# One load instead of three ahead of the opening barrier, in a streaming row-mean on Trainium2

## Chip, cores, metric

The kernel runs on one core of a Trainium2 chip. The metric is device time in microseconds (us). Every run used below was in the fast state, at a granted clock of 1.0. The threshold is 2%.

## The reference

The input is 32 x 512 rows of 1024 floats, 67.11 MB. The output is one float per row.

```python
def reference(x, divisor):          # x: (32, 512, 1024) f32, divisor = 1024.0
    return (np.sum(x, axis=-1) / divisor).astype(np.float32)
```

## The kernel before

The 16384 rows are spread over 128 partitions. Nine tiles of up to 14 rows per partition (128x14x1024 floats, 7168 KB) go through three buffers. All loads are issued from the sync queue. The vector engine (DVE) sums each tile; the activation engine (ACT) takes some rows of the last ones. A tapering tail of small loads keeps the work after the last byte short.

```python
    main = [(14, 0)] * 6 + [(14, 4), (14, 6), (8, 4)]      # (rows, rows summed by ACT)
    bulk = ctx.enter_context(tc.tile_pool(name="bulk", bufs=3))
    # ...
    nc.gpsimd.memset(r, 0.0)
    # ...
    j = 0
    for rows, on_act in main:
        t = bulk.tile([P, 14, D], F32, name="t")
        load(t[:, :rows, :], x_main[:, j : j + rows, :])     # sync queue
        sums(res[:, j : j + rows], t, rows, on_act)
        j += rows
    # ... the tapering tail, scaling, two stores
```

A program has a first block, which ends with a barrier of all engines, and a body. A load in the body is issued after that barrier. The first three loads wait for nothing, since all three buffers are free, so a helper moves them from the body to the place in the first block just before the sync engine's drain:

```python
def start_loads_at_once(nc):
    first, body = nc.main_func.blocks[0], nc.main_func.blocks[1]
    loads = []
    for i in body.instructions:
        if i.engine == SP:
            if type(i).__name__ != "InstDMACopy" or (i.sync_info and i.sync_info.on_wait):
                break
            loads.append(i)
    # ... take them out of the body, then put them ahead of SP's drain:
    first.instructions = first.instructions[:at] + loads + first.instructions[at:]
```

Of the kernel before, what the change touches and what calls it, by code (L numbers as in the profile page):

```python
# [14 lines left out]
SP = mybir.EngineType.SP  # L15


def start_loads_at_once(nc):



    first, body = nc.main_func.blocks[0], nc.main_func.blocks[1]
    loads = []
    for i in body.instructions:
        if i.engine == SP:
            if type(i).__name__ != "InstDMACopy" or (i.sync_info and i.sync_info.on_wait):
                break
            loads.append(i)
    names = {i.name for i in loads}
    assert names  # L30
    body.instructions = [i for i in body.instructions if i.name not in names]
    at = next(
        k for k, i in enumerate(first.instructions) if i.engine == SP and type(i).__name__ == "InstDrain"
    )
    first.instructions = first.instructions[:at] + loads + first.instructions[at:]


def with_sync(i, on_wait=None, on_update=None):
# [29 lines left out]
def close_while_storing(nc, landed):  # L68


    body, end = nc.main_func.blocks[1], nc.main_func.blocks[-1]
    store = [i for i in body.instructions if i.engine == SP and type(i).__name__ == "InstDMACopy"][-1]
    (lane,) = store.sync_info.on_update
    drain = end.instructions[0]
    assert drain.engine == SP and type(drain).__name__ == "InstDrain"
    needs = {w.id: w for w in drain.sync_info.on_wait}
    assert needs[lane.id].wait_value > lane.update_value
    needs[lane.id] = dataclasses.replace(
        needs[lane.id], wait_value=needs[lane.id].wait_value - lane.update_value
    )  # L80

    (done,) = [w for w in store.sync_info.on_wait if w.ant_name.startswith("DVE_")]
    assert needs[done.id].wait_value == done.wait_value
    del needs[done.id]
    own = dict(sync_type="semaphore", id=landed.num, ant_name=landed.name)
    add = mybir.SyncUpdate(update_mode="sem-add-imm", update_value=16, **own)
    sub = mybir.SyncUpdate(update_mode="sem-sub-imm", update_value=16, **own)
    last = nc.sync.wait_ge(landed, 16).ins
    assert nc.main_func.blocks[-1].instructions[-1].name == last.name
    body.instructions = [i for i in body.instructions if i.name != store.name]  # L90
    end.instructions = [
        with_sync(drain, on_wait=tuple(needs.values())),
        with_sync(store, on_wait=(done,), on_update=(add,)),
        *end.instructions[1:-1],
        with_sync(last, on_update=(sub,)),
    ]


@with_exitstack
def kernel(  # L100
    ctx: ExitStack,
    tc: tile.TileContext,
    x: bass.AP,
    divisor: float,
    out: bass.AP,
):
    nc = tc.nc
    landed = nc.alloc_semaphore("landed")
    nc.at_finalize(start_loads_at_once)
    nc.at_finalize(latest_wait_first)  # L110
    nc.at_finalize(lambda nc: close_while_storing(nc, landed))
    xf = x.flatten_outer_dims()
    N, D = xf.shape
    P = nc.NUM_PARTITIONS
    scale = 1.0 / float(divisor)
    J = N // P
    assert J * P == N


    L = 8  # L120
    M = J - L
    x_main = bass.AP(tensor=x.tensor, offset=0, ap=[[M * D, P], [D, M], [1, D]])
    x_last = bass.AP(tensor=x.tensor, offset=P * M * D, ap=[[L * D, P], [D, L], [1, D]])
    o_main = bass.AP(tensor=out.tensor, offset=0, ap=[[M, P], [1, M]])
    o_last = bass.AP(tensor=out.tensor, offset=P * M, ap=[[L, P], [1, L]])


    main = [(14, 0)] * 6 + [(14, 4), (14, 6), (8, 4)]
    last = [(4, 2), (2, 1)]
    assert sum(n for n, _ in main) == M and sum(n for n, _ in last) == L - 2  # L130
    bulk = ctx.enter_context(tc.tile_pool(name="bulk", bufs=3))
    one = ctx.enter_context(tc.tile_pool(name="one", bufs=1))
    psum = ctx.enter_context(tc.tile_pool(name="junk", bufs=4, space=bass.MemoryType.PSUM))

    res = one.tile([P, M], F32, name="res")
    fin = one.tile([P, L], F32, name="fin")
    q = one.tile([P, L], F32, name="q")
    r = one.tile([P, L], F32, name="r")
    nc.gpsimd.memset(r, 0.0)  # L139

    def load(dst, src):
        tc.keep_in_program_order(nc.sync.dma_start(out=dst, in_=src))  # L142

    def act_sum(dst, src, by=1.0):
        n = src.shape[-1]
        junk = psum.tile([P, D], F32, name="junk")
        nc.scalar.activation(junk[:, :n], src, COPY, scale=by, accum_out=dst)  # L147

    def sums(dst, t, rows, on_act):
        d = rows - on_act  # L150
        for i in range(d, rows):
            act_sum(dst[:, i : i + 1], t[:, i, :])
        nc.vector.reduce_sum(out=dst[:, :d], in_=t[:, :d, :], axis=AX)  # L153
# [4 lines that stand above are left out]
        load(t[:, :rows, :], x_main[:, j : j + rows, :])  # L158
# [3 lines that stand above are left out]
    for rows, on_act in last:  # L162
        t = one.tile([P, rows, D], F32, name=f"t{rows}")
        load(t, x_last[:, j : j + rows, :])
        sums(q[:, j : j + rows], t, rows, on_act)
        j += rows


    c = 768
    row = one.tile([P, D], F32, name="row")  # L170
    load(row, x_last[:, j, :])
    act_sum(r[:, j : j + 1], row[:, c:], by=scale)
    nc.vector.reduce_sum(out=q[:, j : j + 1], in_=row[:, :c], axis=AX)  # L173



    a, b = 448, 704
    pa = one.tile([P, a], F32, name="pa")
    pb = one.tile([P, b - a], F32, name="pb")
    pc = one.tile([P, D - b + 2], F32, name="pc")  # L180
    load(pa, x_last[:, L - 1, :a])
    load(pb, x_last[:, L - 1, a:b])
    load(pc[:, : D - b], x_last[:, L - 1, b:])


    nc.gpsimd.tensor_scalar_mul(out=res, in0=res, scalar1=scale)  # L186
    tc.keep_in_program_order(nc.sync.dma_start(out=o_main, in_=res))

    act_sum(pc[:, D - b : D - b + 1], pa)
    nc.vector.reduce_sum(out=pc[:, D - b + 1 :], in_=pb, axis=AX)  # L190
    nc.vector.scalar_tensor_tensor(  # L191
        out=fin[:, : L - 1], in0=q[:, : L - 1], scalar=scale, in1=r[:, : L - 1], op0=MULT, op1=ADD
    )
    scaled = one.tile([P, D - b + 2], F32, name="scaled")
    nc.vector.tensor_scalar(  # L195
        out=scaled, in0=pc, scalar1=scale, scalar2=0.0, op0=MULT, op1=ADD, accum_out=fin[:, L - 1 :]
    )
    tc.keep_in_program_order(nc.sync.dma_start(out=o_last, in_=fin))
# [35 lines left out]
```

## Time and profile before

| | before |
|---|---|
| time, median of the first 3 runs | 161.70 us (161.69 to 161.78) |
| span in the profile | 160.1 us |
| DMA queue busy | 97.8% of 16 engines' span |
| vector engine busy | 75% |
| first reduction starts | 19.58 us |
| reductions of full tiles apart | 16.94 us, of which 15.09 busy |

The lines behind this table are in the prediction. In the view in order of time, a line gives start, duration, engine, source line, operation, output and input; the bracket at its end gives the idle time of the engine just before it and what ended that. Neighbouring lines of one kind are merged: "1.34 ... x3" are three issues, 1.34 us from the start of the first to the end of the last.

Some terms. An issue is the instruction with which the sync queue hands a load to the 16 DMA engines; what it hands over are descriptors. A packet is one record of data moved in the trace (57344 bytes in the full tiles). A completion packet is a record of 4 bytes; each load has 16 of them, taken here to be one per engine. A load has landed when the instruction that waits for it can start, so a landing is dated here by the start of the reduction. The drain (DRAIN) is the sync queue's last instruction before it waits at the barrier. The span runs from the first instruction in the profile to the end of the last.

### The profile page before, as it was taken

The page shows a single profiled execution, that of the slowest core. Times are in us where ns is not written, and L with a number is a line of the kernel's source. Part 1 is how long each engine was busy: PE and PEld are TensorE (multiplying, and loading weights), DVE is VectorE, ACT ScalarE, POOL GpSimd, SP SyncE. Part 2 cuts the span into 40 slices and gives each one's busy share as a digit, 9 for nine tenths or more (in the row PEclk, how much of TensorE's full clock was granted, in tenths as well). Part 3 has the DMA queues.
Part 4 walks back from the last instruction along what each step waited for, and adds up shares of the span by engine and source line. Part 5 has one row for each costly group of instructions (what it writes and reads, how often), then busy time and mean ns, then how long its engine had stood idle before and what let it go on. Part 6 is the DMA issues. An engine that isn't in the chain of part 4 may idle for free.

```text
span 160.1 us, 138 instructions
## 1 busy us (share of the span) xinstructions
DVE 119.9 (75%) x16; ACT 20.7 (13%) x39; POOL 0.8 (1%) x6
## 2 busy tenths in 40 slices
DVE  0000199968998699959995999599987990497985
ACT  3000000000000000000000000000007300491973
POOL 0000000000000000000000000000000000000010
DMA  8899999998899999998899999999799999999993
GB/s 301 387 458 458 458 458 458 458 430 358 358 458 458 458 458 458 458 458 387 358 401 458 458 458 458 458 458 430 315 401 458 458 458 458 393 393 405 415 402 104
DMA packets 2448, 67.18 MB, mean 419 GB/s; under 512 B 528, under 2 KB 912, under 8 KB 1040
## 3 DMA queue, kind: packets, MB, share of 16 engines
q1 hardware_dynamic: 2448, 67.18, 97.8%
HBM read 67.11 MB, written 0.07 MB: 419 GB/s over the span
## 4 chain that ended last, share of the span: by engine, by line
DMA 67%; DVE 29%; another core or an unknown queue 1%; SPq 1%; issue 0%; DVEq 0%
DMA t<-in_x_dram 45%; DVE res L153 28%; DMA row<-in_x_dram 22%; SPq L142 1%; DVE q L173 1%; DVE scaled L195 0%; DVE pc L190 0%; DVE fin L191 0%; DVEq L195 0%; DVEq L229 0%
## 5 line engine op out<-in xcount | busy, mean ns | idle before, releaser
L153 DVE TENSOR_REDUCE res<-t 128x14 f32<-128x14336 f32 (+3 forms) x9 | 114.4, 12716 | 37.9 <-DMA t<-in_x_dram 37.9
L147 ACT ACTIVATE junk<-t 128x1024 f32<-128x1024 f32 x17 | 17.2, 1011 | 135.2 <-DMA t<-in_x_dram 135.2
L153 DVE TENSOR_REDUCE q<-t 128x2 f32<-128x2048 f32 (+1 forms) x2 | 3.5, 1752 | 0.7 <-DMA t<-in_x_dram 0.7
L147 ACT ACTIVATION_READ_ACCUMULATOR junk<-t 128x1 f32 x17 | 3.2, 186 | 0.0
L147 ACT ACT_TABLE_LOAD x1 | 1.3, 1283 | 1.7 <-PEq L215 1.7
L186 POOL TENSOR_SCALAR res<-res 128x120 f32<-128x120 f32 x1 | 0.5, 512 | 150.5 <-DVE res L153 150.5
L173 DVE TENSOR_REDUCE q<-row 128x1 f32<-128x768 f32 x1 | 1.0, 953 | 0.1
L195 DVE TENSOR_SCALAR_CACHE_REDUCE scaled<-pc 128x322 f32<-128x322 f32 x1 | 0.5, 490 | 0.1
L147 ACT ACTIVATE junk<-pa 128x448 f32<-128x448 f32 x1 | 0.5, 547 | 0.1
L190 DVE TENSOR_REDUCE pc<-pb 128x1 f32<-128x256 f32 x1 | 0.4, 412 | 0.0
L147 ACT ACTIVATE junk<-row 128x256 f32<-128x256 f32 x1 | 0.4, 387 | 0.1
L191 DVE SCALAR_TENSOR_TENSOR fin<-q,r 128x7 f32<-128x7 f32 x1 | 0.2, 167 | 0.0
L147 ACT ACTIVATION_READ_ACCUMULATOR junk<-row 128x1 f32 x1 | 0.2, 187 | 0.0
L147 ACT ACTIVATION_READ_ACCUMULATOR junk<-pa 128x1 f32 x1 | 0.2, 186 | 0.0
L139 POOL MEMSET r<- 128x8 f32 x1 | 0.1, 104 | 1.3 <-POOLq L215 1.3
L215 POOL MEMSET const-bfloat16-1.0<- 128x1 bf16 x1 | 0.1, 101 | 0.0
L215 POOL MEMSET const-uint8-127<- 128x1 uint8 x1 | 0.1, 101 | 0.0
L215 POOL MEMSET const-float32-0.0<- 128x1 f32 x1 | 0.1, 99 | 0.2 <-issue 0.2
L215 POOL MEMSET const-float32-1.0<- 128x1 f32 x1 | 0.1, 98 | 0.0
L195 DVE DVE_READ_ACCUMULATOR scaled<-pc 128x1 f32 x1 | 0.1, 82 | 0.0
## 6 DMA issues: line engine op xcount, KB each, us to landing
t<-in_x_dram SPq DMA_DIRECT2D x8, 7168.0 KB, 35.7
t<-in_x_dram SPq DMA_DIRECT2D x1, 4096.0 KB, 28.5
t<-in_x_dram SPq DMA_DIRECT2D x1, 2048.0 KB, 33.0
t<-in_x_dram SPq DMA_DIRECT2D x1, 1024.0 KB, 35.0
row<-in_x_dram SPq DMA_DIRECT2D x1, 512.0 KB, 35.8
pa<-in_x_dram SPq DMA_DIRECT2D x1, 224.0 KB, 36.0
pc<-in_x_dram SPq DMA_DIRECT2D x1, 160.0 KB, 35.7
pb<-in_x_dram SPq DMA_DIRECT2D x1, 128.0 KB, 35.9
```

The source lines that it names most:

```text
L139: nc.gpsimd.memset(r, 0.0)
L142: tc.keep_in_program_order(nc.sync.dma_start(out=dst, in_=src))
L147: nc.scalar.activation(junk[:, :n], src, COPY, scale=by, accum_out=dst)
L153: nc.vector.reduce_sum(out=dst[:, :d], in_=t[:, :d, :], axis=AX)
L173: nc.vector.reduce_sum(out=q[:, j : j + 1], in_=row[:, :c], axis=AX)
L186: nc.gpsimd.tensor_scalar_mul(out=res, in0=res, scalar1=scale)
L190: nc.vector.reduce_sum(out=pc[:, D - b + 1 :], in_=pb, axis=AX)
L191: nc.vector.scalar_tensor_tensor(out=fin[:, : L - 1], in0=q[:, : L - 1], scalar=scale, in1=r[:, : L - 1], op0=MULT, op1=ADD)
L195: nc.vector.tensor_scalar(out=scaled, in0=pc, scalar1=scale, scalar2=0.0, op0=MULT, op1=ADD, accum_out=fin[:, L - 1 :])
L215: nc = _bacc.Bacc("TRN2", target_bir_lowering=False, num_devices=1)
```

## The change

The intent: let only load 1 stand ahead of the barrier. Loads 2 and 3 go back to the head of the body, so the sync engine reaches the barrier earlier and the other engines start earlier. The intent counts on load 2's data not moving anyway while load 1's keeps the DMA engines busy.

```diff
-def start_loads_at_once(nc):
+def start_first_load_at_once(nc):
     first, body = nc.main_func.blocks[0], nc.main_func.blocks[1]
-    loads = []
-    for i in body.instructions:
-        if i.engine == SP:
-            if type(i).__name__ != "InstDMACopy" or (i.sync_info and i.sync_info.on_wait):
-                break
-            loads.append(i)
-    names = {i.name for i in loads}
-    assert names
-    body.instructions = [i for i in body.instructions if i.name not in names]
+    load = next(i for i in body.instructions if i.engine == SP)
+    assert type(load).__name__ == "InstDMACopy" and not load.sync_info.on_wait
+    body.instructions = [i for i in body.instructions if i.name != load.name]
     # ...
-    first.instructions = first.instructions[:at] + loads + first.instructions[at:]
+    first.instructions = first.instructions[:at] + [load] + first.instructions[at:]
     # ... and the one call of the helper, by its new name
```

More of the change, by code (lines that the diff above doesn't have):

```diff
@@ L108 @@
     landed = nc.alloc_semaphore("landed")
-    nc.at_finalize(start_loads_at_once)
+    nc.at_finalize(start_first_load_at_once)
     nc.at_finalize(latest_wait_first)
```

## The prediction

> **What bounds the kernel now.** I read the page from the top: busy shares, the slices, the chain that ended last, and the groups; then the order of time on the vector engine, the stretches between landings, the waits of the queue that issues the loads, and at last the first microseconds, where the change sits.
>
> The busy shares and the chain first.
>
> ```profile
> span 160.1 us, 138 instructions
> DVE 119.9 (75%) x16; ACT 20.7 (13%) x39; POOL 0.8 (1%) x6
> q1 hardware_dynamic: 2448, 67.18, 97.8%
> DMA 67%; DVE 29%; another core or an unknown queue 1%; SPq 1%; issue 0%; DVEq 0%
> ```
>
> The reader is to see that the one DMA queue, q1, has its 16 engines busy 97.8% of the span while the busiest compute engine has 75%. The chain puts 29% on DVE, but that is a way in which it can be followed back, not a limit: it goes through a reduction that freed a buffer, and the buffer was free long before its new data was due. The next two views show this. First the reductions in order of time:
>
> ```profile
> 19.58 15.09 DVE L153 TENSOR_REDUCE res<-t 128x14 f32<-128x14336 f32 x1 [19.58 <-DMA t<-in_x_dram]
> 36.52 15.09 DVE L153 TENSOR_REDUCE res<-t 128x14 f32<-128x14336 f32 x1 [1.86 <-DMA t<-in_x_dram]
> ```
>
> A full tile takes 15.09 us to reduce and the next reduction starts 16.94 us after the one before (36.52 - 19.58). The 1.86 us between are a wait for the load. The stretches between landings say what the load does in that time:
>
> ```profile
> 0.00:4.00 4.00, 0.00 (x0) 1.28 (x1) 0.29 (x5) 1.00 0.89 301
> 4.00:19.58 15.58, 0.00 (x0) 0.00 (x0) 0.00 (x0) 1.00 1.04 453
> 19.58:36.52 16.94, 15.09 (x1) 0.00 (x0) 0.00 (x0) 1.00 1.00 433
> 36.52:53.46 16.94, 15.09 (x1) 0.00 (x0) 0.00 (x0) 1.00 1.00 433
> ```
>
> The last two columns are DMA share and GB/s. Between the first and second landing, and between the second and third, the DMA share is 1.00 at 433 GB/s: no hole. (The 1.04 before is an effect of counting a packet where it starts.) A tile of 7168 KB at 433 GB/s is 16.95 us, the cadence just seen. So from about 4 us on the kernel is a stream of data at a fixed rate. Only three things can set its time: when the stream starts, whether it ever runs dry, and the short tail after the last byte. A change to the opening can touch only the first two.
>
> Now the opening, in order of time:
>
> ```profile
> 0.00 1.34 SPq L142 DMA_DIRECT2D t<-in_x_dram  x3
> 0.32 0.10 POOL L215 MEMSET const-uint8-127<- 128x1 uint8 x1
> 1.74 1.28 ACT L147 ACT_TABLE_LOAD   x1 [1.74 <-PEq L215]
> 1.74 0.10 POOL L139 MEMSET r<- 128x8 f32 x1 [1.32 <-POOLq L215]
> ```
>
> Three issues stand back to back on the sync queue from 0.00 to 1.34 us. The other engines are done with their opening by 0.42 us and then wait at the barrier until 1.74. Last, what belongs to the barrier on the sync queue, from the view of its line:
>
> ```profile
> L215 SPq DRAIN  x1: 125/125/125, 1.4 to 1.4; - x1
> L215 SPq EVENT_SEMAPHORE  x1: 17/17/17, 1.7 to 1.7; - x1
> ```
>
> The sync engine is thus the last to arrive: its drain starts at 1.40 us, right after the third issue, and the barrier opens some 0.15 us after that drain has ended.
>
> **What the Trainium skill says.** The page "DMA: Bandwidth & Descriptors", section "Specifications", gives a fabric ceiling of 435 GB/s for the 16 engines; the trace agrees, with 433 GB/s between landings. The stream has no rate left to gain. The same page, section "Queues, rings and completion order", says that on each DMA engine the descriptors of a row are consumed in ring order. The trace agrees: the three loads, though issued within 1.34 us, are reduced from 19.58, 36.52 and 53.47 us on, one tile of data apart. The second load therefore moves no byte while the first is moving. The same page, section "Latency and other measured facts", gives about 600 ns to the first byte for a load issued from the sync queue. In the trace's records of single packets the first packet of the first load starts at 1.02 us, which is 0.64 us after its issue ended at 0.38.
>
> **The change part by part.** It computes nothing new and removes nothing. In the order of the sync queue it goes from "load 1, load 2, load 3, drain, barrier" to "load 1, drain, barrier, load 2, load 3". Four parts, with single durations from the trace's records.
>
> 1. Load 1. It stays the first instruction of the sync queue, from 0.00 to 0.38 us. Its first packet should start near 1.02 us as before: change 0.
>
> 2. The barrier. Two issues leave its front: load 2 from 0.43 to 0.87 and load 3 from 0.91 to 1.34 us. With the gaps that is 1.34 - 0.38 = 0.96 us. The drain should start at 0.44 instead of 1.40 us, end at 0.56, and the barrier let the engines go at about 0.78 instead of 1.74 us (1.74 - 0.96). The others arrive by 0.42 to 0.49 us (the pool engine's drain took 169 ns from 0.30), so the sync engine stays last, barely. What gains 0.96 us by this: the activation table load, 1.28 us, which would run from 0.78 to 2.06 instead of 1.74 to 3.02, and the memset of r, which is read at 157.6 us. The first activation runs at 121.2 us. DVE has nothing to do before the landing at 19.58. On the path that sets the end: 0.
>
> 3. Loads 2 and 3. Load 2 should be issued at about 0.78 us instead of 0.43: 0.35 us later. Load 3 follows 0.48 us after it, at about 1.26 instead of 0.91. Load 2's data is first wanted when the fastest DMA engine has done its share of load 1. The completion packets of load 1 in the records stand from 18.65 to 19.17 us, so load 2 must be in the ring by 18.65. With 0.64 us from end of issue to first packet it is there by 0.78 + 0.43 + 0.64 = 1.85 us: a margin of some 16.8 us, of which the change spends 0.35. For load 3 the margin is one tile more. On the path: 0.
>
> 4. All later loads wait for a reduction and a buffer, and those follow from the landings, which do not move: 0. The sum is 0.00 us on the path, against a shift of about 0.96 us for things that nobody waits for.
>
> **The rivals.**
>
> A. The first packets get faster. The 16 first packets (one on each DMA engine) start between 1.02 and 1.83 us and take 2.2 to 3.3 us, mean 2.89, where all later ones of 57344 bytes take 2.12. The last engine to get to its second packet does so at 4.38 us, the first at 3.85, and this spread of 0.53 us is still there in the completion packets at 18.65 to 19.17 us, and again one tile later. If writing the descriptors of loads 2 and 3, which falls into the same time, is what slows or staggers the first packets, moving them 0.35 us later could give some of it back: at most the 0.77 us of the first packets' excess, to 160.9 us. Against it: issues of later loads also fall into running packets and hardly touch them. Around the issues at 34.7, 51.6 and 68.6 us the mean packet takes 2.12 us, longer by 0.01 us at most. And load 2 would in the new order still be issued before the first packet starts. That a stream which begins shows the latency of its first reads once is the plainer reading. I give this a gain of 0.1 to 0.4 us one chance in six.
>
> B. The moved loads get in the way. Their descriptors would now be written from about 1.4 to 2.4 us, wholly within the first packets instead of partly ahead of them. If that is what stretches packets, those of the engine that is last could end 0.1 to 0.3 us later, which shifts every landing: to 161.9 or 162.0. The same small effect around later issues speaks against it; some 0.02 us for two issues is what it would support. One chance in eight.
>
> C. The barrier takes the place of the issues and holds load 2 up for long: a late arrival of another engine, or a stall on the way into the main body. It would have to last over 16 us to be seen, and the other engines are at the barrier within half a microsecond. This would make nothing of the time: 161.7.
>
> D. The start of the span shifts, as what is counted first changes. The span begins with the issue of load 1 in the kernel before, and load 1 is in the same place after. The measured 161.7 us is 1.6 us above the span of 160.1, an offset outside it that I take to stay. No change.
>
> **Range and chances.** The central reckoning is 161.7 + 0.00 us. Rival A weighs slightly more than B: 0.17 x (-0.25) + 0.12 x 0.2 is -0.02 us, so 161.7 stays. The three runs before span 0.09 us; another chip or another hour may add two or three tenths. The range 161.2 to 162.1 holds A's and B's usual sizes and that scatter. Two per cent are 3.2 us, four times all that A could return even in full, and no rival reaches that on the slow side. I keep one per cent for faster and two for slower, the latter for some disturbance at start that I do not see.
>
> **What would show it right or wrong.** Right: the first reduction starts at 19.58 us within 0.1, the next ones 16.94 us apart with waits of 1.86; the table load starts near 0.78 us; the sync queue's drain comes after one issue, near 0.44; the DMA share stays at 1.00 between landings. Rival A or B: the first reduction starts 0.1 us or more earlier or later and all later landings move by the same amount, at an unchanged cadence. Rival C: a share under 1.00 between the first and second landing. The prediction would be wrong if the cadence itself moved, for which I see no mechanism, or if the first packet of load 1 started at another time than 1.02 us.

## The result, and the profile after

| | before | after |
|---|---|---|
| median of 4 runs each | 161.69 us | 161.75 us |
| lowest to highest | 161.69 to 161.78 | 161.66 to 161.82 |
| ratio after / before | | 1.0002, 95% interval 0.9985 to 1.0019 |

A ratio here is the mean time of one kernel's fast runs over the mean of the other's fast runs of the same rounds, so it is not quite the ratio of the medians.

The span and the DMA queue of the changed kernel:

```profile
span 160.3 us, 138 instructions
q1 hardware_dynamic: 2448, 67.18, 97.7%
```

The opening of the changed kernel in order of time, with the first two reductions:

```profile
0.00 35.17 SPq L136 DMA_DIRECT2D t<-in_x_dram  x4
0.79 1.28 ACT L141 ACT_TABLE_LOAD   x1 [0.79 <-PEq L209]
0.80 0.10 POOL L133 MEMSET r<- 128x8 f32 x1 [0.38 <-POOLq L209]
19.73 15.09 DVE L147 TENSOR_REDUCE res<-t 128x14 f32<-128x14336 f32 x1 [19.73 <-DMA t<-in_x_dram]
36.65 15.09 DVE L147 TENSOR_REDUCE res<-t 128x14 f32<-128x14336 f32 x1 [1.83 <-DMA t<-in_x_dram]
```

The table load starts at 0.79 us where it stood at 1.74: the barrier opens 0.95 us earlier. Nothing comes of it. The first reduction starts at 19.73 us, which is 0.15 later than in the profile of before, and the second again waits for its load.

The stretches between landings, changed kernel (length, busy time of DVE, ACT and POOL, clock, DMA share, GB/s):

```profile
19.58:36.52 16.94, 15.09 (x1) 0.00 (x0) 0.00 (x0) 1.00 1.00 433
36.52:53.46 16.94, 15.09 (x1) 0.00 (x0) 0.00 (x0) 1.00 1.00 433
```

Rate and share are those of before: no hole was made. The barrier's part on the sync queue, from the view of its line:

```profile
L209 SPq DRAIN  x1: 140/140/140, 0.4 to 0.4; - x1
L209 SPq EVENT_SEMAPHORE  x1: 17/17/17, 0.7 to 0.7; - x1
```

The drain now follows the first issue, at 0.4 us instead of 1.4. By the trace's records of single instructions load 2 is issued at 0.80 us (0.43 before) and load 3 at 1.18 (0.91 before).

One thing in this pair does not fit "nothing moves": the 0.15 us of the first reduction. It runs through to the end (span 160.3 against 160.1). So there were two theories to test.

**Margin theory.** The place of loads 2 and 3 does not matter while they are issued before load 1 leaves the DMA engines without work. The 0.15 us is scatter that each execution draws anew.

**Interference theory** (rivals A and B of the prediction). Descriptors of loads 2 and 3 that are written while the first packets run slow those packets or stagger them, so their place does matter, by some tenths of a us.

A third reading was tried as well: that the reductions, 29% of the chain of waits, are part of what sets the time.

### The profile page after: what moved, and what is told of

The parts are those of the page before. It is cut to its first block, busy times and chain, and to the rows that moved or that the text cites. A ratio compares the mean times of both kernels' runs of the same rounds, so it can differ in the third digit from the quotient of the medians.

```text
span 160.3 us, 138 instructions
## 1 busy us (share of the span) xinstructions
DVE 119.9 (75%) x16; ACT 20.7 (13%) x39; POOL 0.8 (1%) x6
## 4 chain that ended last, share of the span: by engine, by line
DMA 67%; DVE 29%; another core or an unknown queue 1%; SPq 1%; issue 0%; DVEq 0%
DMA t<-in_x_dram 45%; DVE res L147 28%; DMA row<-in_x_dram 22%; SPq L136 1%; DVE q L167 1%; DVE scaled L189 0%; DVE pc L184 0%; DVE fin L185 0%; DVEq L189 0%; DVEq L223 0%
```

## The experiments

Nine runs were made, two of them of the two kernels already known, each in five rounds, on two chips (e1 to e4 on one, e5 to e9 on another); all were correct. Kernels of one batch share nine runs of the kernel before. Their medians were 161.74 us for e1 to e4, 161.74 for e5 to e8 and 161.73 for e9.

### e1_before_again: the kernel before against itself

No edit.

> The kernel before, unchanged, timed against itself. It gives the scatter of the comparison and a second look at the 16 first packets. Margin theory (the place of loads 2 and 3 does not matter while they are issued before the rings run dry near 18.65 us; the spread of the first packets comes out differently in each run by itself): ratio 1.000 within 0.001, first reduction between 19.5 and 19.8 us, the spread of the 16 completion packets of load 1 not again exactly 0.52 us but anywhere from 0.4 to 0.8. Interference theory (the descriptors of loads 2 and 3 set that spread): first reduction again at 19.58 within 0.03 us, spread again near 0.52.

Measured: 161.78 us (161.69 to 162.00), ratio 1.0002, interval 0.9990 to 1.0015. In order of time:

```profile
1.72 1.28 ACT L147 ACT_TABLE_LOAD   x1 [1.72 <-PEq L215]
19.72 15.09 DVE L153 TENSOR_REDUCE res<-t 128x14 f32<-128x14336 f32 x1 [19.72 <-DMA t<-in_x_dram]
```

The unchanged kernel, with all three loads ahead, starts its first reduction at 19.72 us this time, not at 19.58. That is as late as in the changed kernel. The 16 completion packets of load 1 spread over 0.82 us (18.53 to 19.35, a little beyond the 0.8 that was expected at most) against 0.52 in the first profile. The 0.15 us is therefore not a mark of the change.

### e2_after_again: the changed kernel once more

No edit to the changed kernel.

> The changed kernel, unchanged, in five rounds. Margin theory: ratio 1.000 within 0.001, first reduction anywhere from 19.5 to 19.8 us. Interference theory: first reduction again near 19.73 us, spread of the completion packets of load 1 again near 0.71 us against 0.52, and a time longer by about 0.1 us (ratio 1.0007).

Measured: 161.72 us (161.63 to 161.90), ratio 1.0000, interval 0.9986 to 1.0013. In order of time:

```profile
19.63 15.09 DVE L147 TENSOR_REDUCE res<-t 128x14 f32<-128x14336 f32 x1 [19.63 <-DMA t<-in_x_dram]
```

The first reduction starts at 19.63 us and the spread is 0.71. Of the interference theory's figures for this run the spread came out again, but not the landing time and not the longer time. The two orders, two profiles each, give 19.58 and 19.72 against 19.73 and 19.63.

### e3_none_ahead: all three loads behind the barrier

```diff
-    nc.at_finalize(start_first_load_at_once)
```

> No load stands ahead of the opening barrier: all three follow it. Both theories: load 1 is issued when the last other engine has arrived, at an estimated 0.6 to 0.7 us (the pool engine's drain ends at 0.47 us, the barrier took 0.15 us more and 0.07 to the next instruction), every landing moves by that much, and the time grows by 0.5 to 0.7 us to 162.2 to 162.4 (ratio 1.003 to 1.004). If the opening hides a load's start anyway, nothing changes: ratio 1.000.

Measured: 162.42 us (162.27 to 162.72), ratio 1.0042, interval 1.0029 to 1.0055. In order of time:

```profile
0.71 1.28 ACT L140 ACT_TABLE_LOAD   x1 [0.71 <-PEq L208]
0.72 35.08 SPq L135 DMA_DIRECT2D t<-in_x_dram  x4
20.36 15.09 DVE L146 TENSOR_REDUCE res<-t 128x14 f32<-128x14336 f32 x1 [20.36 <-DMA t<-in_x_dram]
```

Load 1 is issued at 0.72 us and its reduction starts at 20.36. The time grows by 0.68 us over the shared median (162.42 - 161.74), which is the delay of that issue within the scatter. (The issue and the time came out 0.02 us above the ranges that were expected.) So the place of load 1 has a price, about one us per us. Moving the other two had none that these runs can see.

### e4_hold_4_rows: loads 2 and 3 only after the first packets

The changed kernel; the pool engine clears part of the second buffer first, so load 2 has to wait for it (the load overwrites what was cleared, so the result stays right).

```diff
         t = bulk.tile([P, 14, D], F32, name="t")
+        if j == 14:
+            nc.gpsimd.memset(t[:, :4, :], 0.0)
         load(t[:, :rows, :], x_main[:, j : j + rows, :])
```

> The changed kernel, with load 2 held back until the pool engine has cleared four rows (128x4096) of its buffer after the barrier, estimated at 3 to 9 us from the opening; load 3 follows it. The first packets of load 1 then run with no other descriptors being written. Margin theory: ratio 1.000 within 0.001, first packets as slow (mean 2.6 to 2.9 us) and as unevenly started as before, spread of completion packets 0.4 to 0.8 us. Interference theory: first packets nearer to 2.12 us, spread clearly under 0.5 us, first reduction at 19.3 us or earlier, time shorter by 0.2 us or more (ratio 0.9985 or lower).

Measured: 161.74 us (161.65 to 162.01), ratio 1.0000, interval 0.9988 to 1.0013. In order of time:

```profile
0.82 3.51 POOL L153 MEMSET t<- 128x4096 f32 x1
19.65 15.09 DVE L147 TENSOR_REDUCE res<-t 128x14 f32<-128x14336 f32 x1 [19.65 <-DMA t<-in_x_dram]
```

The clearing takes 3.51 us and load 2 is issued at 4.36 us, when 12 of the 16 first packets have ended (the last ends at 4.47). These packets still take 2.95 us in the mean, 0.05 more than was expected at most; the last of them still starts late (1.99 us), and the spread of the completion packets is 0.63. With no other load being issued beside them until the very end, the first packets are as slow and as uneven as ever. The interference theory falls here, with one reservation: the clearing itself ran beside these packets. e6 and e7 below take that up.

### e5_hold_18_rows, e6_hold_21_rows, e7_hold_24_rows: how late may load 2 be?

The same edit with longer clearing (4 in the last line for 18 rows in all, 7 for 21, 10 for 24):

```diff
+        if j == 14:
+            nc.gpsimd.memset(t, 0.0)
+            nc.gpsimd.memset(t[:, :4, :], 0.0)
```

> The changed kernel with load 2 (and load 3 behind it) held until the pool engine has cleared 18 rows in the second buffer: four rows took 3.51 us, so the issue of load 2 should stand near 16.7 us. Where the rings are empty, a load lands some 19.6 us after its issue began (kernel with none ahead: issue at 0.72, reduction at 20.36). 16.7 + 19.6 is 36.3 us, just before the 36.6 us at which the second reduction starts anyway. Margin theory: no loss, ratio 1.000 within 0.001. A theory in which the order of issue itself matters, say that a load needs a lead of several us to stream without a hole: a hole between the landings of loads 1 and 2, DMA share under 1.00 there, a time longer by some tenths of a us or more.

> As before with 21 rows: issue of load 2 near 19.3 us, after the rings have run dry at 18.6 to 19.3 us. Margin theory: the second landing moves to 19.3 + 19.6 = 38.9 us, 2.3 us later than in the changed kernel, every later landing by as much, and the time is 164.0 us (ratio 1.014; 1.011 to 1.017). If the vector engine's slack of 1.85 us per tile took up the hole, the loss would be under 0.5 us.

> As before with 24 rows: issue of load 2 near 21.9 us. Margin theory: second landing near 41.5 us, 4.9 us later, time 166.7 us (ratio 1.031; 1.027 to 1.034), that is, beyond the margin each us of delay costs a whole us: 2.6 us more than with 21 rows. If the slack took up part of it: clearly under 2 us more.

| | load 2 issued | second reduction starts | time, median | ratio, 95% interval |
|---|---|---|---|---|
| after (first profile) | 0.80 us | 36.65 us | 161.75 us | 1.0002 (0.9985 to 1.0019) |
| e4, 4 rows | 4.36 | 36.58 | 161.74 | 1.0000 (0.9988 to 1.0013) |
| e5, 18 rows | 16.46 | 36.38 | 161.69 | 1.0000 (0.9987 to 1.0012) |
| e6, 21 rows | 19.02 | 38.66 | 163.69 | 1.0123 (1.0109 to 1.0137) |
| e7, 24 rows | 21.60 | 41.34 | 166.32 | 1.0282 (1.0268 to 1.0296) |

(e6 has four runs in its median, the others five, the changed kernel four.) The clearing was a little faster than estimated, 12.04 us for 14 rows, so the issues came up to 0.3 us before the expected times, and e6's landing and time were 0.2 to 0.3 us under what was expected. The second reduction in e5, e6 and e7, in order of time, with the issue before it in e5 and e7:

```profile
16.46 0.81 SPq L136 DMA_DIRECT2D t<-in_x_dram  x2
36.38 15.09 DVE L147 TENSOR_REDUCE res<-t 128x14 f32<-128x14336 f32 x1 [1.86 <-DMA t<-in_x_dram]
```

```profile
38.66 15.09 DVE L147 TENSOR_REDUCE res<-t 128x14 f32<-128x14336 f32 x1 [4.02 <-DMA t<-in_x_dram]
```

```profile
21.60 0.81 SPq L136 DMA_DIRECT2D t<-in_x_dram  x2
41.34 15.09 DVE L147 TENSOR_REDUCE res<-t 128x14 f32<-128x14336 f32 x1 [6.47 <-DMA t<-in_x_dram]
```

In e5 the vector engine's wait before the second tile is the usual 1.86 us; in e6 it is 4.02 and in e7 6.47. The stretches of e7 show the hole (same columns as above, DMA share and GB/s last):

```profile
4.00:18.00 14.00, 0.00 (x0) 0.00 (x0) 13.94 (x2) 1.00 1.03 446
18.00:22.00 4.00, 2.22 (x1) 0.00 (x0) 3.57 (x1) 1.00 0.00 0
22.00:26.00 4.00, 4.00 (x1) 0.00 (x0) 0.00 (x0) 1.00 1.22 444
```

From 18 to 22 us no data packet starts. What follows is a curve with a knee. Up to an issue at 16.46 us the delay is free. Beyond the knee it costs us for us: from e6 to e7 the issue moves by 2.58 us and the time by 2.63 (166.32 - 163.69). The slack of the vector engine takes up none of it, because what has been lost is time of the stream.

The knee can be worked out from these lines. From issue to reduction a full tile on idle DMA engines takes 19.64 us in e3 (20.36 - 0.72), 19.64 in e6 and 19.74 in e7. The second reduction otherwise starts near 36.6 us. So the estimate for the latest free issue is 36.6 - 19.64, about 17.0 us. The losses agree: e6 and e7 are issued 2.0 and 4.6 us later than that and lose 1.95 and 4.58 us against the shared median. The change under study moved that issue from 0.43 to 0.80.

The packet records of load 2 say what a restart is. In e6 and e7 the DMA engines have run dry, and the 16 first packets of load 2 take 2.83 and 2.89 us in the mean, as slow as those of load 1 at the very start. In e5, where the engines had not run dry, they take 2.14 us, and so do the packets of load 1 that start in the two us before them, from the issue of loads 2 and 3 on. The clearing was over before load 2 was issued, so it did not slow the packets in e6 and e7; and in e4 no other load was issued beside the first packets. What the slow first packets have in common is that the DMA engines start from idle.

### e8_two_ahead: half the change

The kernel before, with a break in its helper after the second load.

```diff
             loads.append(i)
+            if len(loads) == 2:
+                break
```

> Loads 1 and 2 ahead of the barrier, load 3 behind it: half the change. Margin theory: ratio 1.000 within 0.001; the barrier opens near 1.26 us, between the 1.74 and 0.78 us of the two kernels. If the 0.06 us between the two medians of the first comparison were real and due to the moved loads, the time would lie between.

Measured: 161.72 us (161.56 to 161.87), ratio 0.9999, interval 0.9987 to 1.0012. In order of time:

```profile
1.25 1.28 ACT L149 ACT_TABLE_LOAD   x1 [1.25 <-PEq L217]
```

The barrier opens at 1.25 us as reckoned, between the two kernels, and the time does not follow it.

### e9_act_helps: less work for the vector engine

The changed kernel with four rows of each of the first six tiles given to the activation engine.

```diff
-    main = [(14, 0)] * 6 + [(14, 4), (14, 6), (8, 4)]
+    main = [(14, 4)] * 6 + [(14, 4), (14, 6), (8, 4)]
```

> The changed kernel with four of the 14 rows of each of the first six tiles summed by the activation engine, so that the vector engine takes 10.82 us per tile instead of 15.09 (the 128x10 reduction's time). If the reductions were part of what sets the time, as the 29 per cent of the chain of waits may suggest, six tiles of 4.27 us each would return up to 25 us; even one would be 4 us. If the stream of data alone sets it: the vector engine's wait per tile grows from 1.85 to about 6.1 us, the cadence of landings stays at 16.94 us, and the ratio is 1.000 within 0.001.

Measured: 161.93 us (161.86 to 161.94), ratio 1.0012, interval 0.9998 to 1.0026. The busy shares and chain, from the page:

```profile
DVE 94.3 (59%) x16; ACT 46.3 (29%) x87; POOL 0.8 (1%) x6
DMA 72%; DVE 21%; another core or an unknown queue 4%; SPq 1%; issue 0%; DVEq 0%
```

The vector engine's busy time fell from 119.9 to 94.3 us and nothing was gained. In order of time:

```profile
36.64 10.82 DVE L147 TENSOR_REDUCE res<-t 128x10 f32<-128x10240 f32 x1 [6.09 <-DMA t<-in_x_dram]
53.58 10.82 DVE L147 TENSOR_REDUCE res<-t 128x10 f32<-128x10240 f32 x1 [6.12 <-DMA t<-in_x_dram]
```

The reduction became shorter by 4.27 us and the wait before it longer by the same (1.85 to 6.1), with the landings 16.94 us apart as ever. The 29% that the chain gave to DVE had been waiting of another kind, not a bound. The ratio is 0.0002 above the 0.001 that was allowed, and its interval includes 1.000; whether this kernel really loses 0.2 us stays open. It gains nothing, which is what it was for.

### What the ten profiles of a tile-sized load 1 at 0 us say together

The DMA packet records of the traces, for load 1's 16 first packets. (The records do not name the engine; 16 packets run at a time, so the first 16 are taken to be one per engine and the next 16 the second of each.) The last two columns are the start of the first reduction and the time of that same execution less that start, in us. (e6 and e7, where the stream has a hole, end later and have no last entry.)

| profile | last of the 16 first packets starts | mean duration of the 16 | last of the 16 second packets starts | first reduction | time less first reduction |
|---|---|---|---|---|---|
| before | 1.83 | 2.89 | 4.38 | 19.58 | 142.12 |
| e1, before again | 1.65 | 2.94 | 4.56 | 19.72 | 142.10 |
| e8, two ahead | 1.96 | 2.92 | 4.40 | 19.58 | 142.08 |
| after | 2.15 | 2.78 | 4.58 | 19.73 | 142.09 |
| e2, after again | 1.43 | 2.92 | 4.47 | 19.63 | 142.09 |
| e4 | 1.99 | 2.95 | 4.46 | 19.65 | 142.10 |
| e5 | 1.46 | 2.88 | 4.31 | 19.43 | 142.15 |
| e6 | 1.90 | 2.90 | 4.40 | 19.56 | |
| e7 | 2.05 | 2.96 | 4.64 | 19.78 | |
| e9 | 2.07 | 2.85 | 4.56 | 19.72 | 142.14 |

Three readings. The first reduction starts between 19.43 and 19.78 us, in no order that follows the place of loads 2 and 3. It comes 15.12 to 15.20 us after the last second packet starts, in every profile: the first packet that ends last sets it. That is never the one that starts last. In all ten it starts between 1.04 and 1.49 us and takes 2.98 to 3.46 us, while the one that starts last takes 2.11 to 2.59 us and ends before it. And the last column varies by only 0.07 us, while the times of these eight executions vary by 0.28 (161.58 to 161.86). In these profiles, then, nearly all of the scatter from run to run arises in the first 4.6 us, in how late the last of the first packets ends. Why the packets of engines that start from idle are slow, and some slower than others, stays open; e4 to e7 show only that neither the issue of other loads nor the clearing is needed for it.

None of the runs beat the kernel before, and none points to a version that would.

## Why the prediction was right

The time was 161.75 us against the predicted 161.7, within the range. That it came within 0.05 us is luck: runs of one kernel lie up to 0.36 us apart (e4). What is not luck is that nothing on the path moved. Its steps:

1. **Load 1 unmoved.** Right. Its first packet started at 1.03 us against 1.02, and e3 shows that this was the one place that mattered.
2. **The barrier opens 0.96 us earlier and nobody needs it.** Right in size (0.79 us against the reckoned 0.78; 0.95 earlier) and in effect. e8 adds a point halfway with the same time.
3. **Loads 2 and 3 have a large margin.** Right, and shown by e4 to e7 as a curve. The size was a little generous, and its 16.8 us is what the change leaves, not what it takes 0.35 from: the step took load 2 to be in time as long as its first packet is ready at 18.65 us, a margin of 16.8 us. With the knee estimated at 17.0 us and load 2 issued at 0.80, it is 16.2. What the step left out is that a stream which restarts pays for slow first packets (2.83 and 2.89 us in e6 and e7, against 2.12) as well as for the wait to the first byte. Two smaller points: load 3 was issued at 1.18 us and not at 1.26, since the issue of load 2 took 0.33 us here instead of 0.43; and load 2 does move data before all of load 1 is in, from 18.66 us in the profile of before, where the last of load 1 ends at 19.17. It is engine by engine that it comes after load 1.
4. **The sum is 0.** Right within the scatter. The repeated comparisons, 1.0002 for the old order against itself and 1.0000 for the new, cannot tell the two apart. Their intervals are some 0.0013 wide to each side, so the times alone do not exclude a difference under 0.2 us. The time less the first reduction does not show one either: 142.12 and 142.10 us in the old order, 142.09 twice in the new.

The rivals. A and B did not come about in what was tried: with no other load issued beside them (e4), the first packets were unchanged. C, the barrier as a new wait, was there but at the size of 0.37 us for load 2, far under the margin. D held: the offset between time and span was 1.5 to 1.6 us as before.

One of the prediction's own tests was set too tight. It asked for a first reduction at 19.58 us within 0.1, and said that a shift of 0.1 us or more running through all landings would mean A or B. The first profile of the changed kernel showed just this, 0.15 us, and would have been read as B. The second profile of the unchanged kernel showed the same start, 19.72 us. A threshold has to be wider than the scatter of the thing it tests, and one profile does not give that scatter.

## What to carry to other kernels

In a kernel that streams at a fixed rate, ask of an issue order only when the stream starts and whether the queues ever run dry: the issue at the very front is worth its whole delay (0.68 us here), and the next ones are free until the data ahead of them is nearly through (about 17 us here). Opening a barrier earlier gains nothing when every engine behind it waits for that same data. Before a difference of a tenth of a us between two profiles is given a cause, profile the unchanged kernel a second time.

## What the Trainium skill lacked or had wrong

- "DMA: Bandwidth & Descriptors", section "Latency and other measured facts": its figure of about 600 ns to the first byte agrees with the fastest DMA engine here if it is counted from the end of load 1's issue (0.62 to 0.65 us in the ten profiles above; from its start it is 0.99 to 1.03 us), and the page doesn't say from where it counts. Nor does it say there that the 16 engines start unevenly: the last started 1.04 to 1.77 us after that issue ended in before and after, taken twice each, differently in each run. The landing here followed not the last start but the last end of the first packets (4.31 to 4.64 us).
- The same page: I found nothing on the first packets of a stream. Here the 16 first packets of 57344 bytes took 2.78 to 2.96 us in the mean, later ones 2.12, and those after a pause of the stream 2.83 and 2.89 (e6, e7). With the wait for the first byte this is most of what makes a 7168 KB tile take 19.43 to 19.78 us from issue to reduction on idle engines, against 16.94 us from one to the next in a running stream.
- "Runtime: NRT & Kernel Launch", section "The ~15µs preamble/postamble breakdown", prices the runtime's own barrier (355 ns for its round over five engines) but not the program's opening barrier. Here that took 0.22 us from the end of the last engine's drain to the first instruction behind it, in both kernels (1.52 to 1.74 us, 0.57 to 0.79 us).
